# Attention values per head, and their product with the probabilities in two halves of 64 columns, in a float32 decoder layer

## The chip, the cores and the metric

The kernel is one program on one core of a Trainium2 chip. The metric is device microseconds of one execution. Every number below comes from the kernel's profile (one profiled execution) or from its timed runs.

A core has five engines with instruction queues of their own. TensorE (PE) multiplies matrices into PSUM; its weight loads are shown apart as PEld. VectorE (DVE), ScalarE (ACT) and GpSimd (POOL) work on whole tiles, and SyncE (SP) issues most transfers. An engine runs its queue in order, so an instruction that waits holds up all that stand behind it.

## The reference

One decoder layer for 512 tokens of width 1024: a token-mixing sublayer (sparse attention on a latent of rank 128, beside a gated short convolution), and a channel-mixing sublayer (a gated MLP). All data is float32. The attention, cut to what matters:

```python
c_kv  = rms_norm(c_kv, kv_norm_g)                          # (S, 128): latent keys and values
q_lat = einsum('bshd,hrd->bshr', q_att, w_uk)              # queries taken into the latent
...
# per query: score all earlier keys, keep the best 128, softmax over these
logits = einsum('bqhr,bqkr->bqhk', qb, c_sel) * 64 ** -0.5
probs  = softmax(logits)
o_lat  = einsum('bqhk,bqkr->bqhr', probs, c_sel)           # outputs in the latent
...
att = einsum('bshr,hrd->bshd', o_lat, w_uv)                # (S, 8 heads, 64)
merged = sigmoid(g_att + b0) * (att @ w_br_att) + sigmoid(g_conv + b1) * (conv_y @ w_br_conv)
h = layer_norm(ALPHA * h + merged @ w_o)
```

The last product of the attention may be taken in either order: (probs x c) x w_uv, or probs x (c x w_uv).

## The kernel before

**Number format.** Nearly all matrix products are done in `float32r`, with each operand split in a high part and a low part (a rounded copy by ScalarE, and the difference by VectorE or POOL). A product is then three matmuls: high with high, high with low, low with high (`mm3`, lines 153 to 157). `evac_split` (lines 143 to 145) brings a PSUM result to SBUF in this split form: a cast by ScalarE (L144), then a subtraction by VectorE (L145). Products in plain `float32` need no split; the embedding product `ple` (L322) and the transposes (L653) are of that kind.

**Order of work.** The order is the order in which the code is written: there is no scheduler. `plan` fills a list of steps, and each step takes one chunk of weights of 512 KB (`Chunk`): SyncE loads it, ScalarE casts it (L74), VectorE or POOL makes the low part (L141), three steps ahead of its use. `preps` are small pieces of work done before a given step. In the stretch of the attention a step of the gates (`gt`) or branches (`br`) is 24 matmuls of 128 x 512.

**The attention** is woven between these steps. Its heads are in two groups of four (g = 0, 1) and its queries in four blocks of 128 (b = 0 to 3); block b sees (b + 1) x 128 keys. `ATT_AT` (line 90) says ahead of which chunk each attention step n stands, where 0 is the first chunk of the gates. Step n starts block n of the sequence (g, b), and goes on with the blocks before it. On each block run, one step apart:

- `att_a`: logits (`lg`, two heads at a time, each in 64 of the array's rows, L164), masking and maximum by VectorE (L633), exponential with sum by ScalarE (L639), reciprocal and scaling by VectorE (L642, L645). The result is `p`.
- `att_b`: TensorE transposes each 128 x 128 piece of `p` (L653); `evac_split` makes `pT` of it, high and low.
- `att_c`: the latent outputs, `ol` (L663): the keys' rows `ckn` as weights, `pT` as the moving operand, three matmuls of 128 x 512 per 128 keys, for four heads at once; two `evac_split` per block.
- `att_d`: once per group, `at` (L678): `w_uv` as weights, `ol` as the moving operand. The weights of a head are padded with zeros to 128 columns, so that two heads add up into the two halves of one PSUM tile. Then `evac_split`.

`kproj` (L609) makes the keys per head, `kT`, from the transposed latent `ckT`, with weights that `uk_prep` (L602) loads on ScalarE's queue. `topk` runs on VectorE in small pieces beside the steps. `at_step` (L1325) makes POOL's transfers of weight sums wait for a token of VectorE, so that they keep pace with the steps.

Tiles come from pools with a fixed number of buffers: `k4` (28), `k2` (8), and PSUM `ps` (8).

Of the kernel before, what the change touches and what calls it, by code (L numbers as in the profile page):

```python
# [13 lines left out]
P = 128  # L14
# [69 lines left out]
class Kern:  # L84
# [2 lines left out]
    LEAD = 3  # L87
    NK4 = 28
    SIDE_NS = 3600
    ATT_AT = (-2, 0, 2, 4, 6, 7, 8, 10, 12, 13, 14)  # L90

    def __init__(self, ctx, tc, a, out):
        self.ctx, self.tc, self.nc, self.a, self.out = ctx, tc, tc.nc, a, out
# [156 lines left out]
    def start(self):  # L250
# [3 lines left out]
        self.pwdram = [self.dram.tile([P, D], F32, name=f"psp{i}", tag=f"psp{i}") for i in range(3)]  # L254
        pw = [self.k4(f"pws{i}", F32, (P, 2, 512)) for i in range(3)]
        wx = [self.k4(f"wx{i}", F32R, (P, 2, 2, 200)) for i in range(4)]
        self.ckn = self.k4("ckn", F32R, (P, 2, NB, R))
        self.widx = [self.sm("widx", [P, H], bufs=4) for _ in range(NB)]
        rn, cks = {}, {}

# [100 lines left out]
        def small_norm(bs):  # L361

            n = len(bs)
            var = self.sm("kvar", [P, 2, n], bufs=2)
            mvs = []
            for i, b in enumerate(bs):
                o = cks[b]
                sq = self.k2(f"sq{b}")[:, :R]
                nc.scalar.activation(sq, o[:, :R], AF.Square, accum_out=var[:, 0, i:i + 1])
                nc.scalar.mul(self.widx[b], o[:, 192:200], WSCALE)  # L370
                st = self.sm("kst", [P, 6], bufs=2)
                nc.vector.bn_stats(st, o[:, R:R + 64])
                mv = self.sm("kmv", [P, 2], bufs=4)
                nc.vector.bn_aggr(mv, st)
                nc.vector.tensor_scalar(var[:, 1, i:i + 1], mv[:, 1:2], EPS, None, op0=OP.add)
                mvs.append(mv)
            nc.vector.tensor_scalar(var[:, 0], var[:, 0], 1.0 / R, EPS, op0=OP.mult, op1=OP.add)
            r = self.sm("krstd", [P, 2, n], bufs=2)
            rf, vf = (t.rearrange("p a b -> p (a b)") for t in (r, var))
            nc.gpsimd.tensor_tensor(rf, vf, self.neghalf.to_broadcast([P, 2 * n]), op=OP.pow)  # L380
            def rest():
                for i, b in enumerate(bs):
                    o = cks[b]
                    kn = self.k2(f"kn{b}", F32, (P, 3, 64))
                    nc.vector.scalar_tensor_tensor(kn[:, 2], o[:, R:R + 64], mvs[i][:, 0:1], self.kig,
                                                   op0=OP.subtract, op1=OP.mult)
                    for k in range(2):
                        nc.vector.scalar_tensor_tensor(kn[:, k], kn[:, 2], r[:, 1, i:i + 1], self.kib,
                                                       op0=OP.mult, op1=OP.add)
                    cn = self.sm("cn", [P, R], bufs=4)  # L390
                    nc.vector.scalar_tensor_tensor(cn, o[:, :R], r[:, 0, i:i + 1], self.kvg, op0=OP.mult, op1=OP.mult)
                    nc.scalar.copy(self.ckn[:, 0, b], cn)
                    nc.gpsimd.tensor_tensor(self.ckn[:, 1, b], cn, self.ckn[:, 0, b].bitcast(F32), op=OP.subtract)
                    cks[b] = cn, kn

            return rest
# [101 lines left out]
    def plan(self):  # L498
# [100 lines left out]

        self.kT = []  # L600

        def uk_prep():  # L602
            raw = self.k2("wuk_raw")
            nc.scalar.dma_start(raw, a["w_uk"])
            self.wuk = self.k4("wuk", F32R, (P, 2, 512))
            nc.scalar.copy(self.wuk[:, 0], raw)
            nc.gpsimd.tensor_tensor(self.wuk[:, 1], raw, self.wuk[:, 0].bitcast(F32), op=OP.subtract)

        def kproj():  # L609
            for j in range(4):  # L610
                o = self.ps("kT")
                js = slice(j * P, (j + 1) * P)
                self.mm3(o, self.wuk[:, 0, js], self.wuk[:, 1, js], self.ckT[:, 0], self.ckT[:, 1], True, True)
                t = self.k4(f"kT{j}", F32R, (P, 2, S))
                self.evac_split(t[:, 0], t[:, 1], o)
                self.kT.append(t)


        self.olat = {}
        self.attT = []  # L620

        def att_a(g, b):
# [23 lines left out]
            return pt  # L646

        def att_b(g, b, pt):
            res = []
            for c in range(b + 1):  # L650
                t = self.ps("pT")
                for i in range(4):
                    nc.tensor.transpose(t[:, i * P:(i + 1) * P], pt[i // 2][:, i % 2, c * P:(c + 1) * P],  # L653
                                        self.ident)
                d = self.k4(f"pT{g}_{b}_{c}", F32R, (P, 2, S))
                self.evac_split(d[:, 0], d[:, 1], t)
                res.append(d)
            return res

        def att_c(g, b, pTs):  # L660
            o = self.ps("ol")
            for c, d in enumerate(pTs):
                self.mm3(o, self.ckn[:, 0, c], self.ckn[:, 1, c], d[:, 0], d[:, 1], c == 0, c == b)  # L663
            if b == 0:
                self.olat = [[self.k4(f"ol{g}{i}{j}", F32R, (P, 2, S)) for i in range(2)] for j in range(2)]
            tb = slice(b * P, (b + 1) * P)
            o4 = o.rearrange("p (h t) -> p h t", h=4)
            for i in range(2):
                self.evac_split(self.olat[0][i][:, :, tb], self.olat[1][i][:, :, tb], o4[:, 2 * i:2 * i + 2])

        def att_d(g):
            wh, wl = (t.rearrange("p (h d) -> p h d", h=H) for t in (uv.hi, uv.lo))
            for j in range(2 * g, 2 * g + 2):
                o = self.ps("at")
                for i in range(2):
                    h = 2 * j + i
                    xh, xl = (self.olat[k][j % 2][:, i] for k in range(2))
                    self.mm3(o, wh[:, h], wl[:, h], xh, xl, i == 0, i == 1)  # L678
                t = self.k4(f"at{j}", F32R, (P, 2, S))
                self.evac_split(t[:, 0], t[:, 1], o)  # L680
                self.attT.append(t)

        self.att_state = {}
        seq = [(g, b) for g in range(2) for b in range(NB)]

        def att_step(n):

            def f():
                if n - 3 in (3, 7):
                    att_d((n - 3) // 4)  # L690
                if 0 <= n - 2 < len(seq):
                    g, b = seq[n - 2]
                    att_c(g, b, self.att_state.pop(("b", n - 2)))
                if 0 <= n - 1 < len(seq):
                    g, b = seq[n - 1]
                    self.att_state["b", n - 1] = att_b(g, b, self.att_state.pop(("a", n - 1)))
                if 0 <= n < len(seq):
                    g, b = seq[n]
                    while b not in self.ready:
                        next(self.side)  # L700
                    self.att_state["a", n] = att_a(g, b)
            return f


# [135 lines left out]
                fn()  # L840
            return f

        def and_keys(fn):
            def f():
                fn()
                kproj()
            return f

        at_first = len(self.steps)
# [6 lines left out]
        for i, o in enumerate(order):  # L856
            if o[0] == "g":
                w = wa(20 + 2 * o[1] + o[2], lo="p" if i < 16 else "v")
                fn = gate(o[1], o[2], w)
            elif o[0] == "r":  # L860
                w = chunk(a["w_br"][2 * o[1] + o[2]], lo="p" if i < 16 else "v")
                fn = branch(o[1], o[2], w)
            elif o[0] == "q":
                w = wa(4 + o[1], lo="v" if o[1] == 1 else "p")
                fn = qatt(o[1], w)
            else:
                w = wa(8 + 3 * o[1] + "cxb".index(o[0]), lo="p" if i else "v")
                fn = conv(*o, w)
            if i == 8:
                fn = and_keys(fn)  # L870
            ws = [w]
            n = att_at.get(i)
            if n is not None:
                fn = with_att(n, fn)
            if n == 4:
                uv = chunk(a["w_uv"], resident=True)
                ws.append(uv)
            step(fn, ws)
        uv.last = at_first + max(att_at)
        self.side_from = at_first - 1  # L880


# [658 lines left out]
        ws += [chunk(sd["abcd"][kk], resident=kk > 3, cols=1024 if kk < NCH - 1 else 512) for kk in range(NCH - TAILC, NCH)]  # L1541
        for blk in range(2):
            step(tail(blk, ws), ws if blk else ws[NCH - TAILC:])
        self.preps.setdefault(5, []).append(uk_prep)
        nxt = 10 ** 9
        for c in reversed(self.chunks):
            c.due = max(min(c.need - c.lead, nxt - 1 if c.last > c.need else nxt), c.after)
# [42 lines left out]
def _layout(inputs):  # L1590
# [32 lines left out]
    for q in range(4):  # L1623
        k, n = q % 2, q // 2
        r = rows(g["w_ffn_down"][0][k * (DFF // 2):(k + 1) * (DFF // 2), n * 512:(n + 1) * 512])
        for i in range(6):
# [1 line left out]
            down[q, i, :, :t.shape[1]] = t  # L1628
    br = [np.concatenate([col(w, 2 * jj), col(w, 2 * jj + 1)], axis=1)
          for jj in range(4) for w in (g["w_br_att"][0], g["w_br_conv"][0])]  # L1630
    uv = np.zeros((P, H, 2, 64), np.float32)
    for h in range(H):
        uv[:, h, h % 2] = g["w_uv"][0, h]
    vecs = np.zeros((P, NV), np.float32)
    vecs[:, NV_GATE:NV_GATE + 16] = g["b_gate"][0].reshape(16, P).T
    vecs[:, NV_MW:NV_MW + 12] = g["mix_conv_w"][0].reshape(12, P).T
# [7 lines left out]
        "w_a": np.stack(wa), "w_b": np.stack(wb), "w_br": np.stack(br), "w_dn": down,  # L1644
        "w_x": rows(np.concatenate([c_kv, k_idx, w_idx], axis=1)).reshape(P, -1),
        "w_uk": g["w_uk"][0].transpose(1, 0, 2).reshape(P, -1),
        "w_uv": uv.reshape(P, -1),
        "vecs": vecs,
        "ln_emb_g": g["ln_emb_g"], "ln_emb_b": g["ln_emb_b"],
        "ln1_g": g["ln1_g"][0], "ln1_b": g["ln1_b"][0],  # L1650
# [23 lines left out]
```

## Time and profile before

| | |
|---|---|
| timed runs | 744.41, 744.42, 742.76 us (median 744.41) |
| the profiled execution | span 742.6 us, from the first to the last instruction; the page gives no other time of it |
| TensorE busy | 733.0 us, 99% of the span, 4231 matmuls |
| VectorE, ScalarE, POOL busy | 608.9, 413.5 and 241.5 us |
| attention on TensorE | logits from 135.2 us on; transposes 146.8 to 245.8; `ol` 159.4 to 253.9; `at` 210.0 to 262.1 |

How to read the rows that follow: a group's row has the source line, engine, operation, the tile written and the tiles read, the shape and the count; then the busy time in us and the mean of one in ns; then the idle time of the engine just before these instructions, and what ended it. A timeline row has its start and duration in us. A matmul's duration includes its way through the array, so matmuls overlap, and the distance between starts is what one costs in a row of them. A row of waits names the waiting engine and line, what it waited for, the total in us, the number of times and the longest.

### The profile page before, as it was taken

The numbers are of one execution on the slowest core, as the hardware profiler recorded it, in microseconds if no ns is written. First come the engines' busy times: TensorE is split into PE (matmuls) and PEld (weight loads), VectorE is DVE, ScalarE is ACT, GpSimd is POOL, SyncE is SP. The second block draws the span as 40 slices with busy tenths as digits, with TensorE's granted clock in tenths as the row PEclk, the third lists the DMA queues.
The fourth block names the chain that finished last, engine by engine and source line by source line (L and its number), as shares of the span: only waits on it lengthen the run. The fifth ranks groups of instructions, "written<-read, shape, count | busy, mean of one in ns | idle before, by whom it ended". The sixth has DMA issues, their size and how long they took to land.

```text
span 742.6 us, 11858 instructions
## 1 busy us (share of the span) xinstructions
PE 733.0 (99%) x4231; PEld 641.6 (86%) x4231; DVE 608.9 (82%) x1052; ACT 413.5 (56%) x704; POOL 241.5 (33%) x329
## 2 busy tenths in 40 slices
PE   9999999999999999999999999999999999999996
PEld 5998888888888888888888999999999998888885
DVE  5877999876666456979898899899999999978797
ACT  4557424467566435333565666777577765655630
POOL 4313655545523646010101233434332212121002
PEclk9999999999999999999999999999999999999999
DMA  9372598779977999889876998989888968998761
GB/s 353 102 282 100 166 384 286 240 241 246 189 163 156 206 202 297 303 273 355 294 309 201 302 283 256 248 230 237 230 226 241 266 203 220 269 261 253 256 208 66
DMA packets 61866, 178.26 MB, mean 240 GB/s; under 512 B 7232, under 2 KB 7360, under 8 KB 61424
## 3 DMA queue, kind: packets, MB, share of 16 engines
q1 hardware_dynamic: 43392, 138.96, 53.0%
q0 software_dynamic: 17264, 36.31, 27.4%
q10 hardware_dynamic: 1152, 2.25, 0.8%
q8 instruction: 33, 0.54, 0.3%
q14 instruction: 25, 0.20, 0.1%
HBM read 171.72 MB, written 70.78 MB: 327 GB/s over the span
## 4 chain that ended last, share of the span: by engine, by line
PE 89%; DVE 5%; DMA 3%; issue 1%; ACT 1%; DVEq 0%; POOL 0%; POOLq 0%; ACTq 0%
PE ffb L1227 17%; PE dn L1409 5%; PE dn L1410 5%; PE dn L1408 5%; PE gt L155 4%; PE gt L156 4%; PE gt L157 4%; DMA wr<-ws 3%; PE cv L155 2%; PE cv L157 2%; PE cv L156 2%; PE br L155 2%; PE wo L805 2%; PE wo L804 2%; PE br L157 2%; PE br L156 2%
## 5 line engine op out<-in xcount | busy, mean ns | idle before, releaser
L141 DVE TENSOR_TENSOR wl<-wr,wh 128x1024 fp32r<-128x1024 f32 (+1 forms) x172 | 196.7, 1160 | 39.9 <-ACT wh L74 39.1
L74 ACT CAST wh<-wr 128x1024 fp32r<-128x1024 f32 (+1 forms) x183 | 179.0, 987 | 83.2 <-DMA wr<-in_w_dn 12.7
L1335 POOL TENSOR_TENSOR behind<-token,neghalf 128x1 f32<-128x1 f32 x112 | 77.3, 818 | 287.3 <-ACT token L1334 208.7
L1227 PE MATMUL ffb<-hsh,wh 128*128 128x256 f32 x304 | 86.2, 284 | 0.0
L1227 PE MATMUL ffb<-hsl,wh 128*128 128x256 f32 x304 | 86.0, 283 | 0.0
L1227 PE MATMUL ffb<-hsh,wl 128*128 128x256 f32 x304 | 86.0, 283 | 0.0
L1227 PE MATMUL ffb<-h1T,wh 128*128 128x256 f32 x456 | 83.9, 283 | 0.1
L1227 PEld LDWEIGHTS ffb<-h1T,wh 128*128 128x128 f32 x456 | 71.1, 192 | 0.4 <-ACT c L1250 0.3
L1227 PE MATMUL ffb<-h1T,wl 128*128 128x256 f32 x228 | 64.7, 284 | 0.3 <-DVE wl L141 0.3
L1227 PEld LDWEIGHTS ffb<-hsh,wh 128*128 128x128 f32 x304 | 58.3, 192 | 0.2
L1227 PEld LDWEIGHTS ffb<-hsl,wh 128*128 128x128 f32 x304 | 58.4, 192 | 0.0
L1227 PEld LDWEIGHTS ffb<-hsh,wl 128*128 128x128 f32 x304 | 58.4, 192 | 0.0
L155 PE MATMUL gt<-hT,wh 128*128 128x512 f32 x128 | 50.6, 395 | 0.1
L156 PE MATMUL gt<-hT,wh 128*128 128x512 f32 x128 | 49.9, 390 | 0.0
L157 PE MATMUL gt<-hT,wl 128*128 128x512 f32 x128 | 49.8, 389 | 0.0
L1227 PEld LDWEIGHTS ffb<-h1T,wl 128*128 128x128 f32 x228 | 43.7, 192 | 0.7 <-DVE wl L141 0.7
L141 POOL TENSOR_TENSOR wl<-wr,wh 128x1024 fp32r<-128x1024 f32 x15 | 36.2, 2410 | 24.9 <-ACT wh L74 24.6
L173 POOL TENSOR_TENSOR rstd<-veps,neghalf 128x1 f32<-128x1 f32 x12 | 7.1, 590 | 101.6 <-DVE nm L196 67.5
L1200 POOL DMA_DIRECT2D ws<-in_w_a x38 | 36.6, 1536 | 2.0 <-issue 1.3
L1200 POOL DMA_DIRECT2D ws<-ws x38 | 35.5, 1181 | 4.5 <-issue 2.5
L155 PE MATMUL cv<-hT,wh 128*128 128x512 f32 x80 | 31.4, 392 | 0.0
L157 PE MATMUL cv<-hT,wl 128*128 128x512 f32 x80 | 31.1, 389 | 0.0
(342 smaller groups left out, 1977.5 us busy)
## 6 DMA issues: line engine op xcount, KB each, us to landing
wr<-in_w_a SPq DMA_DIRECT2D x61, 512.0 KB, 4.9
ws<-in_w_a SPq DMA_DIRECT2D x76, 256.0 KB, 6.2
wr<-ws SPq DMA_DIRECT2D x38, 512.0 KB, 6.3
ws<-in_w_a POOLq DMA_DIRECT2D x38, 256.0 KB, 8.6
ws<-ws POOLq DMA_DIRECT2D x38, 256.0 KB, 7.9
wr<-in_w_b SPq DMA_DIRECT2D x15, 512.0 KB, 5.5
wr<-in_w_dn SPq DMA_DIRECT2D x15, 512.0 KB, 6.3
wr<-in_w_a SPq DMA_DIRECT2D x19, 256.0 KB, 7.0
```

The lines of the kernel that those rows point to most:

```text
L74: nc.scalar.copy(hi, raw)
L141: (self.nc.vector if eng == "v" else self.nc.gpsimd).tensor_tensor(lo, raw, hi.bitcast(F32), op=OP.subtract)
L155: t.matmul(out, wh, xh, start=start, stop=False)
L156: t.matmul(out, wh, xl, start=False, stop=False)
L157: t.matmul(out, wl, xh, start=False, stop=stop)
L804: nc.tensor.matmul(o, act[:, 0, tb], wl, start=False, stop=False, skip_group_check=not check)
L1200: return lambda: nc.gpsimd.dma_start(to, what, accum_op=OP.add, max_dma_last_dim=4096)
L1227: nc.tensor.matmul(o, l[:, c], r, start=start and c + i == 0, stop=stop and c == 3 and i == 2, skip_group_check=True)
L1335: nc.gpsimd.tensor_tensor(self.sm("behind", [P, 1], bufs=2), t, self.neghalf, op=OP.mult)
L1408: nc.tensor.matmul(o, ah, wh[:, i, c], start=first, stop=False, skip_group_check=free)
L1409: nc.tensor.matmul(o, ah, wl[:, i, c], start=False, stop=False, skip_group_check=free)
L1410: nc.tensor.matmul(o, al, wh[:, i, c], start=False, stop=last, skip_group_check=free)
```

## The change

The values are made once per head from the latent, `vl` = c x w_uv, by `vproj`, as `kproj` makes the keys: it runs behind the chunk at position 10, the keys' at 8. The weights w_uv no longer come as a chunk with zeros, but as 256 KB on ScalarE's queue (`latent_prep`). The latent outputs (`ol`), the keys' rows in two parts (`ckn`) and the product with the padded weights are gone. The transposed probabilities are copied by ScalarE in plain float32, without a split, into tiles that hold two query blocks side by side (256 columns), except where the last keys are seen by one block only (128). A new `att_c` runs once per group: for two heads, two halves of the queries and each 128 keys, the weights are 64 columns of `vl`, and the output is 64 of the 128 partitions of a PSUM tile, so that two heads stand side by side. These matmuls are plain float32. The places of the attention steps are new, and there is one step fewer.

```diff
-    ATT_AT = (-2, 0, 2, 4, 6, 7, 8, 10, 12, 13, 14)
+    ATT_AT = (-2, 0, 2, 4, 6, 8, 9, 10, 12, 14)
...
-                    nc.scalar.copy(self.ckn[:, 0, b], cn)
-                    nc.gpsimd.tensor_tensor(self.ckn[:, 1, b], cn, self.ckn[:, 0, b].bitcast(F32), op=OP.subtract)
...
+        def latent_prep(name):
+            def f():
+                raw = self.k2(f"{name}_raw")
+                nc.scalar.dma_start(raw, a[name])
+                w = self.latent_w[name] = self.k4(name, F32R, (P, 2, 512))
+                nc.scalar.copy(w[:, 0], raw)
+                nc.gpsimd.tensor_tensor(w[:, 1], raw, w[:, 0].bitcast(F32), op=OP.subtract)
+            return f
...
+        def vproj():
+            w = self.latent_w["w_uv"]
+            for c in range(NB):
+                o = self.ps("vl")
+                cs = slice(c * P, (c + 1) * P)
+                self.mm3(o, self.ckT[:, 0, cs], self.ckT[:, 1, cs], w[:, 0], w[:, 1], True, True)
+                if c % 2 == 0:
+                    t = self.k4(f"vl{c}", F32, (P, 2, S))
+                nc.scalar.copy(t[:, c % 2], o)
+                self.vals.append(t[:, c % 2])
...
         def att_b(g, b, pt):
...
-                d = self.k4(f"pT{g}_{b}_{c}", F32R, (P, 2, S))
-                self.evac_split(d[:, 0], d[:, 1], t)
-                res.append(d)
+                if c == b and b % 2:
+                    pv[c, b // 2] = self.k2(f"pT{g}_{b}_{c}", F32, (P, 4, P))
+                elif (c, b // 2) not in pv:
+                    pv[c, b // 2] = self.k4(f"pT{g}_{b}_{c}", F32, (P, 4, 2 * P))
+                at = slice(0, P) if c == b else slice(b % 2 * P, b % 2 * P + P)
+                nc.scalar.copy(pv[c, b // 2][:, :, at], t.rearrange("p (h t) -> p h t", h=4))
...
+        def att_c(g):
             for j in range(2 * g, 2 * g + 2):
                 o = self.ps("at")
+                for half in range(2):
+                    for c in range(2 * half + 2):
+                        for i in range(2):
+                            x = self.pv[g][c, half][:, 2 * j - 4 * g + i]
+                            n = x.shape[-1]
+                            h = 2 * j + i
+                            nc.tensor.matmul(o[64 * i:64 * i + 64, 256 * half + 256 - n:256 * half + 256],
+                                             self.vals[c][:, 64 * h:64 * h + 64], x,
+                                             start=c == 0, stop=c == 2 * half + 1, skip_group_check=True)
                 t = self.k4(f"at{j}", F32R, (P, 2, S))
                 self.evac_split(t[:, 0], t[:, 1], o)
                 self.attT.append(t)
...
         def att_step(n):
             def f():
-                if n - 3 in (3, 7):
-                    att_d((n - 3) // 4)
-                if 0 <= n - 2 < len(seq):
-                    g, b = seq[n - 2]
-                    att_c(g, b, self.att_state.pop(("b", n - 2)))
+                if n in (5, 9):
+                    att_c(n // 9)
...
-            if i == 8:
-                fn = and_keys(fn)
+            if i in (8, 10):
+                fn = and_latent(fn, kproj if i == 8 else vproj)
...
-            if n == 4:
-                uv = chunk(a["w_uv"], resident=True)
-                ws.append(uv)
-            step(fn, ws)
+            step(fn, [w])
...
-        self.preps.setdefault(5, []).append(uk_prep)
+        for n, name in ((5, "w_uk"), (8, "w_uv")):
+            self.preps.setdefault(n, []).append(latent_prep(name))
```

What this makes of the order is shown at two places. The first is TensorE in attention step 5. In the rows `ol`, `at` and `lg` are the PSUM tiles written, `pT_2_1` with a number behind it is the transposed probabilities of query block 2 and key block 1, and the shape is partitions x columns of the output. Before, the end of the block's latent outputs, then the next transposes and logits:

```order
L155 MATMUL ol_2413<-pT_3_2_2317,ckn 128x512
L156 MATMUL ol_2413<-pT_3_2_2317,ckn 128x512
L157 MATMUL ol_2413<-pT_3_2_2317,ckn 128x512
L155 MATMUL ol_2413<-pT_3_3_2325,ckn 128x512
L156 MATMUL ol_2413<-pT_3_3_2325,ckn 128x512
L157 MATMUL ol_2413<-pT_3_3_2325,ckn 128x512
L653 MATMUL pT_2430<-ident_95,p_0_0_2330 128x128 x2
L653 MATMUL pT_2430<-ident_95,p_0_1_2331 128x128 x2
L164 MATMUL lg_2442<-kT_1490,qa_1208 128x256
```

Now, at the same step, the second of the group's two pairs of heads, then transposes and logits as before:

```order
L686 MATMUL at_2441<-pT_0_0_1813,vl_1603 64x256 x2
L686 MATMUL at_2441<-pT_1_1_1968,vl_1603 64x128 x2
L686 MATMUL at_2441<-pT_2_0_2112,vl_1603 64x256 x2
L686 MATMUL at_2441<-pT_2_1_2119,vl_1603 64x256 x2
L686 MATMUL at_2441<-pT_2_2_2126,vl_1614 64x256 x2
L686 MATMUL at_2441<-pT_3_3_2287,vl_1614 64x128 x2
L667 MATMUL pT_2457<-ident_95,p_0_0_2291 128x128 x2
L667 MATMUL pT_2457<-ident_95,p_0_1_2292 128x128 x2
L164 MATMUL lg_2468<-kT_1486,qa_1204 128x256
```

Each "x2" row of `at` is one matmul for each of two heads, into the two halves of the partitions; the rows of `ol` ahead of the transposes are gone at the other steps too.

The second place is ScalarE from attention step 5 to step 6. Here `wh` is a cast of a chunk of weights, `sig` a gate's sigmoid, `p` the exponentials, and ACT_TABLE_LOAD changes between the tables of sigmoid and exponential. Before:

```order
L144 CAST pT_0_0_2435<-pT_2430 128x512
L639 ACT_TABLE_LOAD
L639 ACTIVATE p_1_0_2440,sums_2439<-p_1_0_2440,nmx_2462 128x256 x2
L639 ACTIVATE p_1_1_2441,sums_2439<-p_1_1_2441,nmx_2462 128x256 x2
L74 CAST wh_2474<-wr_2045 128x1024
L144 CAST at_2532<-at_2525 128x512
L144 CAST at_2542<-at_2535 128x512
L144 CAST ol_2549<-ol_2545 128x2x128
L144 CAST ol_2550<-ol_2545 128x2x128
L144 CAST pT_1_0_2562<-pT_2557 128x512
L144 CAST pT_1_1_2570<-pT_2565 128x512
L639 ACTIVATE p_2_0_2575,sums_2574<-p_2_0_2575,nmx_2597 128x384 x2
```

Now:

```order
L144 CAST at_2454<-at_2441 128x512
L674 COPY pT_0_0_2462<-pT_2457 128x4x128
L653 ACT_TABLE_LOAD
L653 ACTIVATE p_1_0_2466,sums_2465<-p_1_0_2466,nmx_2488 128x256 x2
L653 ACTIVATE p_1_1_2467,sums_2465<-p_1_1_2467,nmx_2488 128x256 x2
L74 CAST wh_2500<-wr_2168 128x1024
L781 ACT_TABLE_LOAD
L781 ACTIVATE sig_2531<-gt_2380,vec_79 128x512
L781 ACTIVATE sig_2531<-gt_2506,vec_79 128x512
L674 COPY pT_0_0_2462<-pT_2549 128x4x128
L674 COPY pT_1_1_2560<-pT_2555 128x512
L653 ACT_TABLE_LOAD
```

The casts of `ol` between the steps are gone, the casts of `at` stand ahead of step 5's exponentials instead of ahead of step 6's, and a gate's sigmoids, with a table load on each side of them, now stand between the exponentials of steps 5 and 6.

More of the change, by code (lines that the diff above doesn't have):

```diff
@@ L256, in start @@
         wx = [self.k4(f"wx{i}", F32R, (P, 2, 2, 200)) for i in range(4)]
-        self.ckn = self.k4("ckn", F32R, (P, 2, NB, R))
         self.widx = [self.sm("widx", [P, H], bufs=4) for _ in range(NB)]
@@ L600, in plan @@
         self.kT = []
[L602 to L607, printed above, removed]
+        self.latent_w = {}
+        def latent_prep(name):
[6 more added lines that the diff above has]
+            return f
         def kproj():
+            wuk = self.latent_w["w_uk"]
             for j in range(4):
@@ L612, in kproj @@
                 js = slice(j * P, (j + 1) * P)
-                self.mm3(o, self.wuk[:, 0, js], self.wuk[:, 1, js], self.ckT[:, 0], self.ckT[:, 1], True, True)
+                self.mm3(o, wuk[:, 0, js], wuk[:, 1, js], self.ckT[:, 0], self.ckT[:, 1], True, True)
                 t = self.k4(f"kT{j}", F32R, (P, 2, S))
@@ L616, in kproj @@
                 self.kT.append(t)
-        self.olat = {}
+        self.vals = []
+        def vproj():
[8 more added lines that the diff above has]
+                self.vals.append(t[:, c % 2])
         self.attT = []
@@ L648, in att_b @@
         def att_b(g, b, pt):
-            res = []
+            pv = self.pv.setdefault(g, {})
             for c in range(b + 1):
@@ L654, in att_b @@
                                         self.ident)
-                d = self.k4(f"pT{g}_{b}_{c}", F32R, (P, 2, S))
-                self.evac_split(d[:, 0], d[:, 1], t)
-                res.append(d)
[L658 to L672, printed above, removed]
+                if c == b and b % 2:
[5 more added lines that the diff above has]
+        def att_c(g):
             for j in range(2 * g, 2 * g + 2):
                 o = self.ps("at")
[L675 to L678, printed above, removed]
+                for half in range(2):
[7 more added lines that the diff above has]
+                                             start=c == 0, stop=c == 2 * half + 1, skip_group_check=True)
                 t = self.k4(f"at{j}", F32R, (P, 2, S))
@@ L681, in att_d @@
                 self.attT.append(t)
-        self.att_state = {}
+            del self.pv[g]
+        self.att_state, self.pv = {}, {}
         seq = [(g, b) for g in range(2) for b in range(NB)]
@@ L688, in f @@
             def f():
-                if n - 3 in (3, 7):
-                    att_d((n - 3) // 4)
-                if 0 <= n - 2 < len(seq):
-                    g, b = seq[n - 2]
-                    att_c(g, b, self.att_state.pop(("b", n - 2)))
+                if n in (5, 9):
+                    att_c(n // 9)
                 if 0 <= n - 1 < len(seq):
                     g, b = seq[n - 1]
-                    self.att_state["b", n - 1] = att_b(g, b, self.att_state.pop(("a", n - 1)))
+                    att_b(g, b, self.att_state.pop(n - 1))
                 if 0 <= n < len(seq):
@@ L700, in f @@
                         next(self.side)
-                    self.att_state["a", n] = att_a(g, b)
+                    self.att_state[n] = att_a(g, b)
             return f
@@ L841, in with_att, with and_latent @@
             return f
-        def and_keys(fn):
+        def and_latent(fn, proj):
             def f():
                 fn()
-                kproj()
+                proj()
             return f
@@ L868, in plan @@
                 fn = conv(*o, w)
-            if i == 8:
-                fn = and_keys(fn)
-            ws = [w]
+            if i in (8, 10):
+                fn = and_latent(fn, kproj if i == 8 else vproj)
             n = att_at.get(i)
@@ L874, in plan @@
                 fn = with_att(n, fn)
-            if n == 4:
-                uv = chunk(a["w_uv"], resident=True)
-                ws.append(uv)
-            step(fn, ws)
-        uv.last = at_first + max(att_at)
+            step(fn, [w])
         self.side_from = at_first - 1
@@ L1630, in _layout @@
           for jj in range(4) for w in (g["w_br_att"][0], g["w_br_conv"][0])]
-    uv = np.zeros((P, H, 2, 64), np.float32)
-    for h in range(H):
-        uv[:, h, h % 2] = g["w_uv"][0, h]
     vecs = np.zeros((P, NV), np.float32)
@@ L1646, in _layout @@
         "w_uk": g["w_uk"][0].transpose(1, 0, 2).reshape(P, -1),
-        "w_uv": uv.reshape(P, -1),
+        "w_uv": g["w_uv"][0].transpose(1, 0, 2).reshape(P, -1),
         "vecs": vecs,
```

## The prediction

> **What bounds the kernel now.** I read the page first: the busy times and the shares of the chain that ended last.
>
> ```profile
> span 742.6 us, 11858 instructions
> PE 733.0 (99%) x4231; PEld 641.6 (86%) x4231; DVE 608.9 (82%) x1052; ACT 413.5 (56%) x704; POOL 241.5 (33%) x329
> PE 89%; DVE 5%; DMA 3%; issue 1%; ACT 1%; DVEq 0%; POOL 0%; POOLq 0%; ACTq 0%
> ```
>
> TensorE is busy 99% of the span and carries 89% of the chain. A busy TensorE may still hide waits, so next the busy time by stretches (columns: stretch, length, then PE, PEld, DVE, ACT, POOL, the granted clock, the DMA share, GB/s) and TensorE's waits over the whole run.
>
> ```profile
> 67.00:119.00 52.00, 52.00 (x230) 43.05 (x230) 46.76 (x113) 23.22 (x38) 35.09 (x20) 1.00 0.66 234
> 160.00:263.00 103.00, 102.47 (x523) 84.08 (x522) 61.28 (x191) 63.17 (x122) 50.37 (x100) 1.00 0.92 200
> 416.00:477.00 61.00, 61.00 (x511) 61.00 (x510) 57.45 (x84) 40.62 (x79) 21.76 (x29) 1.00 0.92 259
> 477.00:550.00 73.00, 72.57 (x598) 71.81 (x597) 67.68 (x100) 52.52 (x104) 29.44 (x39) 1.00 0.87 232
> ...
> PE lg L164 <- DVE pT L145: 0.4, 1, 0.4
> ```
>
> In the attention stretch (160 to 263) TensorE stands still for 0.5 us, of which 0.4 is one wait of the logits for VectorE's split of the transposed probabilities. In the later stretches VectorE and the DMA engines are nearly full too, but TensorE is full first, at full clock. So the change is worth what it takes off TensorE's queue, plus or minus new waits there.
>
> **What it removes.** The latent products (`ol`) are 20 groups of three, 60 matmuls; the projection (`at`) is 24 (first the groups of the stretch, by form: busy us, mean ns, idle before; then two rows of the timeline: start, duration).
>
> ```profile
> L155 PE MATMUL ol<-pT,ckn 128*128 128x512 f32 x20 | 7.8, 389 | 0.0
> L155 PE MATMUL at<-ol,wh 128*128 128x512 f32 x8 | 3.1, 389 | 0.0
> L155 PEld LDWEIGHTS ol<-pT,ckn 128*128 128x128 f32 x20 | 3.8, 188 | 0.8
> ...
> 200.31 0.39 PE L155 MATMUL ol<-pT,ckn 128*128 128x512 f32 x1
> ...
> 202.80 0.39 PE L157 MATMUL ol<-pT,ckn 128*128 128x512 f32 x1
> ```
>
> The 389 ns includes the pipeline; the rhythm counts: twelve start within 202.80 - 200.31 = 2.49 us, eleven steps, 0.226 us each. 84 x 0.226 = 19.0 us leave TensorE's queue.
>
> **What it adds.** Twelve matmuls of the same form for the values (`vl`): 12 x 0.226 = 2.7 us. Then 48 plain float32 matmuls, 64 columns of weights each, per head four with 256 moving columns and two with 128. Plain float32 exists in this trace in the embedding product at the start (its weight loads keep its rhythm) and in the transposes; matmuls that share the array exist in the logits, which use 64 rows each (rows of the timeline; the last is from the chain, where 1.75 us is the time that sixteen held it).
>
> ```profile
> 7.07 0.19 PEld L322 LDWEIGHTS ple<-wple,pT 128*128 128x128 f32 x1 [0.24 <-issue]
> ...
> 10.93 0.19 PEld L322 LDWEIGHTS ple<-wple,pT 128*128 128x128 f32 x1 [0.24 <-issue]
> ...
> 176.41 1.66 PE L164 MATMUL lg<-kT,qa 64*128 64x512 f32 x12
> 177.99 0.51 PE L155 MATMUL br<-cvT,wh 128*128 128x512 f32 x1
> ...
> 244.36 1.75 PE pT L653 x16
> ```
>
> The twelve `ple` instructions appear as 24 records: a plain float32 matmul takes two passes. Nine passes of 512 columns take 3.86 us, 0.429 each, so a pass of 256 takes 0.214; for 128 I take the transposes' 1.75/16 = 0.109. One head costs 4 x 2 x 0.214 + 2 x 2 x 0.109 = 2.15 us, eight heads 17.2 us one after another.
>
> Whether two heads side by side run at once no row shows, since no matmul before uses half the columns. The nearest rows are the logits, in half the rows: twelve of 512 take 177.99 - 176.41 = 1.58 us, where twelve in a row would take 2.72, a factor of 0.58. Bounds for the 48: 8.6 us (perfect pairing) to 17.2 (none), or 17.6 with a change of the array's shape per block, which in the logits costs 1.58 - 1.36 = 0.22. I take 9.4, between 8.6 + 2 x 0.22 = 9.0 and 0.58 x 17.2 = 10.0, because the logits are the nearest row. TensorE's own work then changes by -19.0 + 2.7 + 9.4 = -6.9 us.
>
> The Trainium skill has numbers on column pairs: TensorE: Matmul & The Clock Gate, Part 3, gives a measured 2.38x for three column tiles side by side, 0.79 of ideal; on that estimate the 48 would take 17.2/1.59 = 10.8 and the sum would be 1.4 us worse. No run here shows it yet.
>
> **What it does to waits.** VectorE and ScalarE lose work in the stretch, which cannot shorten a time TensorE sets, except for the 0.4 us wait.
>
> ```profile
> L145 DVE TENSOR_TENSOR pT<-pT,pT 128x512 fp32r<-128x512 f32 x20 | 12.7, 685 | 1.6 <-ACT pT L144 1.2
> L145 DVE TENSOR_TENSOR ol<-ol,ol 128x256 fp32r<-128x256 f32 x16 | 6.8, 424 | 13.9 <-ACT ol L144 13.5 <-issue 0.4
> ```
>
> But the removed matmuls also stood between one step's logits and the next step's transposes, and hid the softmax. In the new table of places attention steps 4 and 5 stand two chunks apart, but 5, 6 and 7 stand on consecutive chunks, with nothing on TensorE between the logits of one and the transposes of the next except 24 matmuls, 5.4 us. The softmax's length is read here for step 5 (256 keys) and, without a table load in the chain, for a step with 384 keys like step 6 (rows of the timeline).
>
> ```profile
> 165.61 0.55 DVE L633 CUSTOM_DVE_ANT_0 p<-lg,madd 128x384 f32<-128x384 f32 x1
> ...
> 170.60 1.41 DVE L645 TENSOR_SCALAR p<-p,rs 128x384 f32<-128x384 f32 x4
> ...
> 203.56 0.98 PE L164 MATMUL lg<-kT,qa 64*128 64x256 f32 x12
> ...
> 205.60 0.41 DVE L633 CUSTOM_DVE_ANT_0 p<-lg,madd 128x256 f32<-128x256 f32 x1
> ...
> 207.33 1.28 ACT L639 ACT_TABLE_LOAD   x1 [2.38 <-DVE nmx L636]
> ...
> 210.96 1.14 DVE L645 TENSOR_SCALAR p<-p,rs 128x256 f32<-128x256 f32 x4
> ...
> 213.44 1.04 PE L653 MATMUL pT<-ident,p 128*128 128x128 f32 x8
> ```
>
> Step 5: from VectorE's first reduction to the last scaling 212.10 - 205.60 = 6.5 us. Now the reduction starts about when the logits end (the splits of `ol` and `pT` ahead of it are gone, two splits of `at` stand there instead). The transposes come 5.4 us later and need the four heads one by one: about 0.9 us of wait. Step 6: 172.01 - 165.61 = 6.4, plus 1.28 for the table load that now stands between maximum and exponential: 7.7 us, from about 0.3 before the logits' end, with part of the later transposes still to come: about 1.6 us. Bounds: 0, if the chain is tighter than these rows, and 5.6 if it starts as late as at 203.56 (2.0 us later, both times). I take 2.5, less the 0.4 that goes: +2.1.
>
> **What costs nothing.** The values' weights come on ScalarE's queue ahead of a cast, as the keys' weights did (the tile's own rows, and what ended ScalarE's idle time before them).
>
> ```profile
> L606 ACT CAST wuk<-wuk_raw x1: 620/620/620, 66.7 to 66.7; 128x512 fp32r<-128x512 f32 x1
> L607 POOL TENSOR_TENSOR wuk<-wuk_raw,wuk x1: 1769/1769/1769, 67.4 to 67.4; 128x512 fp32r<-128x512 f32 x1
> ...
>   DMA wuk_raw<-in_w_uk: 2.1, 1
> ```
>
> ScalarE would stand for about 2.1 us, then cast (0.6), POOL subtract (1.8), and ScalarE later copy four times 0.6 for `vl`. In 67 to 119 ScalarE is idle 28.8 us and POOL 16.9; weights are prepared three chunks ahead. If that cover went, the values' 2.7 us would start late by at most 4.5 us; I set 0. The chunk of 512 KB that leaves SyncE's queue frees 1 us of casting at most; 0 too. The removed splits of the keys' rows (`ckn`) lie early, off TensorE's path.
>
> **Sum.** -19.0 + 2.7 + 9.4 + 2.1 = -4.8 us. The page has a span of 742.6 and no other time of that execution; the runs shown are 0.2 to 1.8 above it, median 744.41. Against the span 737.8, against the median 739.6.
>
> **Rivals.**
>
> *The two heads don't overlap.* The 48 matmuls cost 17.6: -19.0 + 2.7 + 17.6 + 2.1 = +3.4, 747.8: slower. For it: no row shows column halves, and each head's two passes use the same half, so the overlap must be between one head's second pass and the other's first. Against it: the logits' 0.58. It decides from 14.2 us on for the 48, 0.83 of one after another. Without new waits it would be +0.9, 745.3.
>
> *The weight loads show.* If a load for one head cannot run under the other head's matmul, 96 loads come on top. From the row of 188 ns for 128 columns, half for 64, that is 9.0 us: 748.6. Against it: the `ol` loads run in the same rows as their matmuls and hide inside 0.226 us. The Trainium skill, TensorE: Matmul & The Clock Gate, Part 3, speaks for it: loads overlap running matmuls only in a different row group, and two heads side by side share all rows; the `ol` rows disagree at full width.
>
> *The waits give the gain back.* At 5.6 us instead of 2.5: 742.7. The DMA engines, 0.92 busy in the stretch, could add to it when steps get shorter. Against the latter: SyncE's loads wait for buffers, not the casts for loads.
>
> ```profile
> SPq L54 <- DVE wl L141: 92.0, 16, 14.2
> ```
>
> *The later stages swallow it.* VectorE has 57.45 of 61 us and 67.68 of 73 there; if they ran by a pace that doesn't move, the time would stay at 744.4. Against it: their loads are issued by chunks, which move with TensorE.
>
> **How the numbers follow.** Forecast (737 to 742): 0.60, because everything in it but the pairing is counted from rows. More gain, no new waits and perfect pairing (-8.1, 736.3): 0.06. Waits give it back: 0.12. Swallowed later: 0.04. No overlap 0.13, loads that show 0.05. The range of 8 in 10 goes from 736.0, the bound of the gain, to 746.5, which takes in the two middle rivals and the no-overlap case with few waits; the likeliest case alone is 737 to 742. About 0.3%, 2.2 us, is what a measurement of this kernel can tell from no change: faster 0.70 (forecast, more gain, a third of the waits), same 0.18, slower 0.12.
>
> **What would show it.** Right: the `at` group has 96 records, each block of 48 spans 4.5 to 5 us with neighbours overlapping in time; `ol` is gone; `vl` costs 2.7 us; transposes wait for VectorE's scaling twice, 1 to 2 us each, and nowhere else. Wrong: a block that spans 8.6 us (no overlap) or has gaps at its loads; waits over 3 us at steps 6 or 7; a cast waiting for a load; TensorE idle after 416.

## The result, and the profile after

| | time, median of the runs | span of the profiled execution |
|---|---|---|
| before | 743.92 us (742.76 to 744.42, 4 runs) | 742.6 us |
| after | 736.87 us (736.74 to 736.92, 4 runs) | 735.1 us |

The ratio is 0.991, with a 95% interval of 0.9896 to 0.9924: 7.05 us less, where 4.8 were forecast. Over 27 further runs of the kernel before its median is 743.12 (742.58 to 744.83), so the better figure for the gain is 6.3 us. The median of 737.9 us given below for the order two and two counts one execution of 4125.39 us; the median of its other three is 737.8.

First the page of after: span, busy times and shares of the chain that ended last. Then four stretches, with the columns as in the prediction.

```profile
span 735.1 us, 11836 instructions
...
PE 725.5 (99%) x4255; PEld 633.8 (86%) x4255; DVE 590.1 (80%) x1015; ACT 409.9 (56%) x688; POOL 243.4 (33%) x326
...
PE 98%; DVE 1%; ACT 1%; issue 0%; DVEq 0%; POOL 0%; POOLq 0%; ACTq 0%
```

```profile
67.00:119.00 52.00, 52.00 (x231) 43.07 (x230) 46.72 (x112) 23.83 (x38) 36.09 (x21) 1.00 0.70 238
160.00:256.00 96.00, 95.36 (x544) 75.90 (x542) 41.09 (x154) 55.65 (x102) 51.55 (x100) 1.00 0.96 205
416.00:477.00 61.00, 61.00 (x510) 61.00 (x510) 59.29 (x85) 40.80 (x79) 21.50 (x29) 1.00 0.94 266
477.00:550.00 73.00, 73.00 (x611) 73.00 (x610) 69.98 (x105) 53.59 (x105) 29.91 (x40) 1.00 0.89 240
```

TensorE sets the time as before: 99% busy, 98% of the chain, full clock. In the attention's stretch VectorE is now busy 41.09 of 96 us (61.28 of 103 before), and TensorE stands still for 0.64. In the later stretches it doesn't stand still at all, though VectorE and the DMA engines are as full as they were.

The new work by its tiles (x count: shortest, median and longest in ns, first and last start in us), and the chain around the new block:

```profile
L686 PEld LDWEIGHTS at<-pT,vl x96: 133/137/138, 203.3 to 255.6; 128*64 128x64 f32 x96
L686 PE MATMUL at<-pT,vl x96: 272/379/431, 203.3 to 255.7; 128*64 128x256 f32 x64, 128*64 128x128 f32 x32
...
L157 PE MATMUL vl<-w_uv,ckT x4: 389/389/390, 130.2 to 132.2; 128*128 128x512 f32 x4
L606 ACT CAST w_uv<-w_uv_raw x1: 627/627/627, 85.9 to 85.9; 128x512 fp32r<-128x512 f32 x1
L607 POOL TENSOR_TENSOR w_uv<-w_uv_raw,w_uv x1: 1327/1327/1327, 90.5 to 90.5; 128x512 fp32r<-128x512 f32 x1
```

```profile
203.33 4.48 PE at L686 x48
...
214.97 1.43 PE pT L667 x8
...
223.50 0.43 DVE p L659
223.98 0.99 PE pT L667 x3
224.97 1.20 PE pT L667 x9
...
251.50 4.48 PE at L686 x48
```

There are 96 records for 48 matmuls, two passes each, in two blocks of 4.48 us. Behind them the eight transposes of step 5's probabilities take 1.43 us, and the twelve of step 6's follow VectorE's scaling (`p`) and are spread over 2.19. (Here and below a wait goes by the step of its softmax, as in the prediction; the transposes themselves stand one step later.) The waits of TensorE in this stretch are one row:

```profile
PE pT L667 <- DVE p L659: 0.6, 1, 0.6
```

### The profile page after: what moved, and what is told of

Its sections match the earlier page's. It is cut to its first block, busy times and chain, and to the rows that moved or that the text cites. A ratio compares the mean times of both kernels' runs of the same rounds, so it can differ in the third digit from the quotient of the medians.

```text
span 735.1 us, 11836 instructions
## 1 busy us (share of the span) xinstructions
PE 725.5 (99%) x4255; PEld 633.8 (86%) x4255; DVE 590.1 (80%) x1015; ACT 409.9 (56%) x688; POOL 243.4 (33%) x326
## 4 chain that ended last, share of the span: by engine, by line
PE 98%; DVE 1%; ACT 1%; issue 0%; DVEq 0%; POOL 0%; POOLq 0%; ACTq 0%
PE ffb L1230 26%; PE dn L1412 5%; PE dn L1413 5%; PE dn L1411 5%; PE gt L155 4%; PE gt L157 4%; PE gt L156 4%; PE cv L155 3%; PE cv L157 2%; PE cv L156 2%; PE wo L812 2%; PE wo L811 2%; PE wo L813 2%; PE br L155 2%; PE br L156 2%; PE br L157 2%
## 5 line engine op out<-in xcount | busy, mean ns | idle before, releaser
L1338 POOL TENSOR_TENSOR behind<-token,neghalf 128x1 f32<-128x1 f32 x112 | 79.6, 846 | 276.8 <-ACT token L1337 209.7
L1230 PE MATMUL ffb<-hsl,wh 128*128 128x256 f32 x304 | 86.1, 283 | 0.0
L1230 PE MATMUL ffb<-hsh,wl 128*128 128x256 f32 x304 | 86.1, 283 | 0.0
L1230 PE MATMUL ffb<-hsh,wh 128*128 128x256 f32 x304 | 86.1, 283 | 0.0
```

The lines of the kernel that those rows point to most:

```text
L1230: nc.tensor.matmul(o, l[:, c], r, start=start and c + i == 0, stop=stop and c == 3 and i == 2, skip_group_check=True)
L1338: nc.gpsimd.tensor_tensor(self.sm("behind", [P, 1], bufs=2), t, self.neghalf, op=OP.mult)
```

## The experiments

**The stalls in the later stage.** From the first to the last matmul of `ff`, between which the blocks (`ffb`) stand, before took 230.5 us and after 229.0 by the rows that follow. So 1.5 of the 7.5 us between the two spans came from a stage that the change doesn't touch. The first run asks whether these stalls belong to the kernel.

> The kernel before, unchanged, in further executions. In the profiled execution of before, the channel-mixing stage by blocks (from the first ff matmul to the last dn) took 1.55 us longer than in after, because TensorE stood still at four places between 478 and 561 us. If those stalls belong to the kernel (theory A), they come again in this profile with about the same sum (1 to 2 us) at the same places. If they are chance (theory B: transfers that land a little late in one execution), their places and sum change, between 0 and 3 us, and the times spread by as much, from about 742.5 to 744.5.

It took 743.12 us (742.48 to 743.88, 10 runs). The rows of `ff` of the profiled execution of before, of the same kernel again, and of after (first and last start):

```profile
L155 PE MATMUL ff<-h1T,wh x48: 389/389/396, 399.2 to 629.7; 128*128 128x512 f32 x48
```

```profile
L155 PE MATMUL ff<-h1T,wh x48: 389/389/396, 399.2 to 628.2; 128*128 128x512 f32 x48
```

```profile
L155 PE MATMUL ff<-h1T,wh x48: 388/389/396, 392.9 to 621.9; 128*128 128x512 f32 x48
```

And of the second execution of before the page, and the stretch in which the first one's TensorE was busy 72.57 of 73 us:

```profile
span 741.4 us, 11858 instructions
...
PE 96%; DVE 2%; DMA 1%; ACT 1%; issue 0%; SPq 0%; POOL 0%; DVEq 0%; ACTq 0%
```

```profile
477.00:550.00 73.00, 73.00 (x610) 73.00 (x610) 68.54 (x103) 54.20 (x106) 28.84 (x40) 1.00 0.91 241
```

In the second execution of before the stage took 229.0 us, as in after, TensorE is busy for all of 477 to 550, and the chain is 96% TensorE instead of 89%. Theory B holds: the stalls come and go between executions of one kernel. The fair comparison of spans is 741.4 against 735.1, 6.3 us, as in the medians.

**The same question from the other side.**

```diff
                 if n in (5, 9):
                     att_c(n // 9)
+                if n == 9:
+                    o = self.ps("fill")
+                    for _ in range(60):
+                        nc.tensor.transpose(o[:, :P], self.ident, self.ident)
```

> The kernel after, with 60 transposes of 128 x 128 into an unused tile behind the last block of values, 60 x 0.109 = 6.5 us of TensorE's time, so that all later stages start when they started in before. If the 1.5 us that after gained beyond the count in the channel-mixing stage hang on when this stage starts (theory A), they are lost again: 736.9 + 6.5 + 1.5 = 744.9, with stalls of TensorE between 478 and 561 us. If they don't (theory B: chance, or another part of the change such as the buffers or the transfers that are gone), 743.4, and TensorE stands still for less than 0.3 us behind 400 us.

It took 743.65 us (743.05 to 744.34, 11 runs), near the 743.4 of theory B, 1.2 below the 744.9 of theory A.

```profile
L155 PE MATMUL ff<-h1T,wh x48: 389/389/396, 399.7 to 629.1; 128*128 128x512 f32 x48
...
PE ffb L1234 <- DVE wl L141: 0.2, 1, 0.2
```

The stage now starts when it did in before and takes 229.4 us, with one short stall. A late start doesn't bring the 1.5 us back.

> The kernel after, unchanged, in further executions, for the spread of its times and a second profile. If the channel-mixing stage by blocks is free of stalls because of the change, it takes 229.6 us from the first ff to the first dn again and all times lie within 0.3 us of 736.9. If its stalls are chance, as those of before (231.2 us in one profile, 229.6 in another), some executions are 0.5 to 1.5 us slower and the median stays within 0.5 of 736.9.

It took 736.70 us (736.53 to 737.34, 4 runs), and `ff` runs from 393.0 to 622.0, 229.0 us, again. That is neither all within 0.3 us of 736.9 nor 0.5 to 1.5 slower, so the spread doesn't tell chance from cause here, and neither profile of after has the stalls. A kernel further down that differs from it in the order of 48 matmuls only has them, so the new attention as such doesn't keep them out.

**Do the two heads run at once?** The same matmuls, one head's twelve ahead of the other's:

```diff
-                for half in range(2):
-                    for c in range(2 * half + 2):
-                        for i in range(2):
+                for i in range(2):
+                    for half in range(2):
+                        for c in range(2 * half + 2):
```

> The kernel after, with the twelve matmuls of one head issued before the twelve of its neighbour: same instructions, same operands, other order. If the gain rests on two heads running at once in the two column halves, each block of 48 records goes from 4.48 us to about 8.6 (17.2 us for both by the count of passes), the whole to 736.9 + 8.3 = 745.2. If neighbouring heads didn't overlap, or if the overlap were one between the passes of one head, nothing changes: 736.9 within 0.5.

It took 741.86 us (741.64 to 742.96, 10 runs), ratio to before 0.9985 (0.9976 to 0.9994): 5.0 us more than after, all of it in the two blocks.

```profile
203.38 7.02 PE at L686 x48
...
254.09 7.02 PE at L686 x48
```

Twice 7.02 - 4.48 = 5.1 us. So the order matters, and the gain rests on the two heads side by side; but the block isn't the 8.6 us expected. Why not is seen in the starts of its first records, in ns from the block's start, read from the trace. The records don't name the head; it is told by the rhythm, and by the durations: 272 ns for 128 columns, 379 for 256, and 431 or 430 where a head starts anew.

```
one head alone     0  267  483  592  701  917 1133 1349
the first head     1565        1780        1996        2105
the second head    1570        1838        2054        2163
one head alone  2272 2488 2704 2920
```

One head alone moves by 216 ns for 256 columns and 109 for 128, the prices of the prediction. The second head starts at 1570, although four passes of the first, which stand ahead of it in the program, are still to start or have just started. For these four passes the heads run together. So the second head's fifth pass starts at 2272 instead of 2864 (2105 + 109, and four passes of its own, 216 + 216 + 109 + 109), 0.59 us earlier, and it is so at each of the three changes of head in a block. Four heads one after another would take 4 x 2.16 + 0.15 = 8.8 us (0.15 is what after's block of 4.48 takes above its passes in pairs, 4.33): 8.8 - 3 x 0.59 = 7.0.

**How far ahead?** That gave a rule with numbers: each column half works through its own passes, and up to four passes can be sent ahead of what runs. Two more orders test it.

```diff
-                    for c in range(2 * half + 2):
-                        for i in range(2):
+                    for c, i in ((c, i) for d in range(half + 1) for i in range(2) for c in (2 * d, 2 * d + 1)):
```

> The kernel after, with the matmuls of the two heads alternating by twos: two of one head, then two of its neighbour. Theory A: the two column halves of the array work through their own matmuls, and up to four passes (two plain float32 matmuls) can be sent ahead of the pass that runs, as the run with one head after another shows, where the next head's first pass began with four passes of the former still to come. Then two and two overlap as fully as one and one: a block stays at 4.5 us, the whole at 736.9. Theory B: only direct neighbours run at once; then every second matmul is alone, a block takes about 6.5 us, and the whole is 736.9 + 4 = 741.

And, in the second half of the queries, four of one head ahead of four of the other:

```diff
-                    for c in range(2 * half + 2):
-                        for i in range(2):
+                    for i in range(2):
+                        for c in range(2 * half + 2):
```

> The kernel after, with two matmuls of one head and then two of its neighbour in the first half of the queries, but four and four in the second half. With four passes sent ahead (theory A) a walk through the order gives 5.4 us for a block, 1.07 more than for heads that alternate, so 4.48 + 1.07 = 5.55 us and 736.9 + 2.1 = 739.0 in all. With three passes ahead it would be 6.05 + 0.14 = 6.2 us and 740.3; if only direct neighbours overlap (theory B), near the 7.0 us of one head after another and 741.9.

The chain's rows of the first and of the second:

```profile
203.63 4.53 PE at L686 x48
...
251.83 4.53 PE at L686 x48
```

```profile
203.35 5.72 PE at L686 x45
...
252.73 5.72 PE at L686 x45
```

Two and two take 4.53 us (4.5 expected), four and four 5.72 (5.55 expected): theory A. Theory B's 6.5 and 7.0 are out. In the walk through the order each half runs its own passes in turn, at 216 and 109 ns, and a pass is sent when fewer than four of those ahead of it are sent and not yet started. By it, three passes ahead would give 7.35 us for one head after another, more than the 7.02 measured, and five would give 6.06 and, for four and four, 4.98. Four fits best; it gives 6.71, 4.33 and 5.41 us for the three orders, and the 0.2 to 0.3 us above that lie at the block's ends and where a head starts anew (267 ns instead of 216).

In whole time four and four took 739.82 us (739.34 to 740.73), 739.0 expected and 739.4 by its blocks. Two and two took 737.9 (median of the runs), 1.0 above what its blocks give, and its profile shows where that comes from:

```profile
471.00:544.00 73.00, 72.72 (x603) 72.23 (x602) 68.54 (x103) 54.07 (x105) 28.78 (x39) 1.00 0.90 240
...
L155 PE MATMUL ff<-h1T,wh x48: 389/389/396, 393.3 to 623.2; 128*128 128x512 f32 x48
```

These are the stalls of before again: the first two begin 82.6 and 86.1 us behind the first `ff` in both traces. They fall on some executions of kernels with either attention: of the nine profiled ones, before has three, two and two has two, the late start has one, and the other six have none. TensorE waits there for a split of weights (the first row, of before), and the split for a load. In the chain of two and two a load is on its way for 8.93 us, and ScalarE's cast follows it (second fence); in after the same cast follows its load too (third fence), but 76.5 us behind the first `ff` instead of 78.2.

```profile
PE ffb L1227 <- DVE wl L141: 0.3, 2, 0.2
```

```profile
462.52 8.93 DMA wr<-ws
...
471.52 1.06 ACT wh L74
```

```profile
469.37 1.05 ACT L74 CAST wh<-wr 128x1024 fp32r<-128x1024 f32 x1 [0.71 <-DMA wr<-ws]
```

That load is issued 69.2 to 69.4 us behind the first `ff` in all nine executions. By the landings in the traces it lands at 78.2 us in before and in two and two, and at 76.1 to 77.3 us in the other seven, which have no stall there. So the load takes longer, and isn't issued later. Why it takes longer in some executions no run here shows. It isn't shown either that the order of the 48 matmuls has no part in it: three of the times of two and two, 737.22 to 738.0, lie at or above the upper end of after's eight, 736.53 to 737.34.

**The waits.** The last experiment moves the steps apart.

```diff
-    ATT_AT = (-2, 0, 2, 4, 6, 8, 9, 10, 12, 14)
+    ATT_AT = (-2, 0, 2, 4, 6, 7, 9, 11, 13, 14)
```

> The kernel after with other places for the attention's steps 5, 6, 7 and 8: chunks 7, 9, 11, 13 instead of 8, 9, 10, 12, so that the softmaxes of 256, 384 and 512 keys have two chunks of matmuls over them and the short one of 128 keys has one. If the new waits of TensorE for the softmax (0.6 us at step 6, and about 0.55 us by which the transposes of step 5 are stretched) come from the places, they go: 736.9 - 1.2 = 735.7. If the short softmax, with a table load of 1.3 us in it, isn't covered by one chunk and the block of 4.5 us, a wait of 0.5 to 1 us comes at step 5 instead and it is 736.5. If VectorE's work at the later chunks is what counts, no change: 736.9.

It took 734.98 us (734.48 to 735.61, 4 runs): ratio to before 0.989 (0.9877 to 0.9904), and 1.9 us below after, where 1.2 were expected.

```profile
215.22 0.87 PE pT L667 x8
...
228.46 1.31 PE pT L667 x12
...
160.00:254.00 94.00, 94.00 (x544) 75.94 (x542) 41.36 (x154) 55.98 (x103) 50.07 (x99) 1.00 0.97 207
```

TensorE no longer stands still in the stretch, and the transposes run at their own pace: 0.87 instead of 1.43 us at step 5, 1.31 instead of 2.19 at step 6. With the gap of 0.64 that is 0.56 + 0.88 + 0.64 = 2.1 us; from the first logits to the first branch the two traces differ by 2.05. My 1.2 had counted the gap and step 5, and missed that the twelve transposes of step 6 were paced by VectorE's scaling too. This version is faster than both kernels.

## Why the prediction was right, and by how much it was off

| step | forecast, us | measured, us |
|---|---|---|
| `ol` and `at` in three parts go | -19.0 | -19.1 (13.64 + 5.44 by the starts in the trace) |
| `vl` comes | +2.7 | +2.8 (first logits at 138.05 instead of 135.26) |
| 48 matmuls in pairs | +9.4 | +9.3 (2 x 4.48, and 0.3 in the rows beside them) |
| new waits | +2.5 | +2.1 |
| waits that go | -0.4 | -1.4 |
| sum | -4.8 | -6.3; the spans of undisturbed executions differ by 6.3 |

- **The sum.** The forecast stood at 739.6, from a median of 744.41; the runs of after have 736.87. The time came out faster, as forecast, inside the range and 0.1 below the likeliest case's own 737 to 742. Of the 2.7 us between forecast and median, 1.3 lie in the base (744.41, against 743.12 over the 27 further runs) and 1.5 in the change; both err to the same side. (The forecast named 737.8 against the span, too. Where a run has both on record, its time is 1.8 above its span: 736.87 and 735.1, 743.19 and 741.4.)
- **Pairing.** Right. Two heads side by side run as fast as one: a block takes 4.48 us, its passes in pairs 4.33, so the bound of 8.6 was nearer than the logits' factor of 0.58. The surcharge is there all the same, and most of it stands beside the blocks. By the starts in the traces the gates ahead of the two blocks take 0.09 and 0.06 us more than without a block behind them, the four transposes behind the first 0.06 more, and the 96 branches behind the second 0.13 more (21.89 instead of 21.76). With these 0.3 us the blocks cost 9.3, where 9.4 were forecast.
- **New waits.** Right in place, and in size at step 6: forecast 1.6, measured 0.64 + 0.88 = 1.5. At step 5 it is 0.56, where 0.9 were forecast. The bound of 5.6 doesn't follow from its own terms (2.5 and twice 2.0 are 6.5), but no sum rests on it except that rival's. A table load stands between maximum and exponential in both softmaxes, as the forecast had it:

```profile
210.82 1.28 ACT L653 ACT_TABLE_LOAD   x1 [1.80 <-DVE nmx L650]
...
219.46 1.28 ACT L653 ACT_TABLE_LOAD   x1 [0.78 <-DVE nmx L650]
```

  The wait at step 5 isn't in the list of waits: its eight transposes are stretched.
- **Waits that go: the step that was mis-sized.** I took the 0.4 us that the waits' view names. But a wait between the matmuls of a block lengthens the block by more than the idle time shown, since the matmuls' ends, which are modelled, cover part of it. Rows of before that I did not lay side by side show it: twelve logits of 128 columns start at 192.89, and the next matmul comes at 194.74, 1.85 us later, while the same twelve take 0.81 where nothing is in their way.

```profile
192.89 0.88 PE L164 MATMUL lg<-kT,qa 64*128 64x128 f32 x7
194.14 0.55 PE L164 MATMUL lg<-kT,qa 64*128 64x128 f32 x5 [0.37 <-DVE pT L145]
194.74 0.50 PE L155 MATMUL gt<-hT,wh 128*128 128x512 f32 x1
```

```profile
135.26 0.81 PE lg L164 x12
...
161.17 1.53 PE lg L164 x11
```

  The second fence is from the chain of before; its second row is a block of 384 columns. In after the same two blocks take 1.27 and 0.82 us:

```profile
163.28 1.27 PE lg L164 x11
...
191.41 0.82 PE lg L164 x12
```

  Over the eight blocks of logits it is 10.58 us before and 9.14 after, by the starts in the trace. The plain copies of `pT` have no subtraction behind them, so the logits no longer wait for it. The row of 0.37 us names that wait for the block at 192.89; for the shorter stretch of the one at 161.17 (1.53 instead of 1.27) no view names a wait, and that it has the same cause is not shown.
- **What costs nothing.** Right: the weights of the values were ready at 91.8 us (90.5 + 1.3), 38 us ahead of their use at 129.7, and TensorE is busy for all of 67 to 119.
- **The base.** The sum was made against an execution that held 1.2 us of chance stalls (span 742.6; 741.4 without). The four runs of before beside the result have a median of 743.92, 0.8 above that of the 27 further runs, so part of the measured 7.05 is no gain.
- **Rivals.** *No overlap* is out by the 4.48 us, and the run with one head after another shows that even then only 7.0 of 8.8 would have been paid. *Loads that show* is out: 96 loads of 137 ns leave no trace in the rhythm, not even beside pairs of passes of 109 ns. The Trainium skill, TensorE: Matmul & The Clock Gate, Part 3, has loads overlap running matmuls only in a different row group; the two heads share all 128 rows, and the measurement decides against the rule here. *Waits that give the gain back* took 2.1, not 5.6. *Swallowed later* is out: `ff` takes 229.0 us at either start, in the executions without stalls. A cast does wait for a load there, which the prediction named as a sign of being wrong (0.71 us in the row of after above), but TensorE isn't idle for it.

## What to carry to other kernels

Two products in plain float32 with 64 output rows each shared the array's columns here for the price of one, as long as their matmuls stood within four passes of each other in the program; put them one and one or two and two. When work leaves an engine's queue, look both ways: for what it covered (the softmax here, won back by placing steps two chunks apart) and for blocks that are longer than the same block elsewhere, because a wait inside a block shows whole in its length and only in part in the list of waits. And profile the base twice before a sum of a few us is made against it.

## What the runs showed of the hardware that was not expected

- TensorE starts passes out of the program's order when they belong to different column halves: the second head's first pass at 1570 ns, ahead of three of the first head's that start at 1780, 1996 and 2105. The Trainium skill (the same page, Part 3, The mechanism) says that matmuls start in strict program order; for these passes the trace disagrees. So what stands at the head of this text, that an engine runs its queue in order, doesn't hold for them either.
- A plain float32 pass of 64 output columns costs 216 ns for 256 moving columns and 109 for 128, the same as the 128-column ones of the prediction; two in the two halves cost as much as one, a factor of 1.93 over both blocks (17.3 us by these prices, 8.96 measured).
